# One row of statistics for the feed-forward: a product of ones with 256 columns, and a power on GpSimd over the row

## The chip, the cores and the metric

The kernel runs on one core of a Trainium2 chip. The metric is the device time of one execution in microseconds, the median of several. The engines are TensorE (PE in the rows, PEld for its weight loads), VectorE (DVE), ScalarE (ACT), GpSimd (POOL) and SyncE (SP), which issues transfers here.

## The reference

Two models run one after the other on 256 tokens of width 1024. The first has two layers, each with a feed-forward, a mixer of three branches and a second feed-forward; the second model has two layers of another mixer. The change touches the four feed-forwards:

```python
def rms_norm(x, g):
    y = xf * lax.rsqrt(jnp.mean(xf * xf, axis=-1, keepdims=True) + EPS)
    return (y * g.astype(jnp.float32)).astype(x.dtype)

def swiglu(h, w1, w3, w2):
    return (jax.nn.silu(h @ w1) * (h @ w3)) @ w2

for l in range(DEPTH):
    x = x + 0.5 * swiglu(rms_norm(x, ffn1_norm[l]), ffn1_w1[l], ffn1_w3[l], ffn1_w2[l])
    ...
    x = x + 0.5 * swiglu(rms_norm(x, ffn2_norm[l]), ffn2_w1[l], ffn2_w3[l], ffn2_w2[l])
```

Everything is float32.

## The kernel before

The activations lie transposed: `xT` has 128 channels on the partitions, in 8 chunks, and the 256 tokens as columns. A product in near float32 is made of three matmuls: `xh`, `xl` are the high part and the remainder of the activations, `H`, `L` those of the weights.

Weights arrive as slabs of 128x1024 in five buffers `raw`, issued by SyncE. For each slab ScalarE makes `H` (L329) and VectorE makes `L = raw - H` (L333), with three buffers each, about two slabs ahead of TensorE. One slab gives 24 matmuls of 256 columns (L429 to L431: `H` with `xh`, `H` with `xl`, `L` with `xh`).

The feed-forward (`ffn`) has 22 blocks `f`. Each takes two slabs, one for the columns of `w1` and one for those of `w3`, into one PSUM tile (`col2`); a task `gated` then makes `t = p * rb` on VectorE (L589), `u = silu(t)` on ScalarE (L591), `w = p * u` on VectorE (L594), and the high part and remainder `gh`, `gl` of it. So the factor 1/rms of each token, `rb`, is multiplied in only after the product, and TensorE can start before it is known. The first three or four blocks use PSUM tiles of the pool `pa`, so that several can wait for `rb`; the others use `pd`.

`rb` is a 128x256 tile, the same row of 256 factors on all partitions. `stats` makes it from `ss`, the sums of squares per partition and token: a product with one column of ones for each half of the tokens (L477), the mean and epsilon on VectorE (L480, `ms`), a power of -0.5 on GpSimd for 128x2 numbers (L481, `m`), two diagonal matrices `dg` on VectorE (L486), their products with a matrix of ones (L490), and a copy to SBUF on ScalarE (L492, `rb`). The mixers use `m` too; the feed-forward uses `rb` alone.

The order on each engine is the order in which the Python code issues instructions; nothing reorders it. Tasks are generators: `spawn` puts one in a list with a delay, `tick` (called after every four chunks of a product) runs the tasks that are due, and `yield n` puts a task off by n ticks. `gated` waits in this list, and not on an engine, until the task of the statistics has ended; from then on it issues at most one block every two ticks.

Of the kernel before, what the change touches and what calls it, by code (L numbers as in the profile page):

```python
# [14 lines left out]
OP = mybir.AluOpType  # L15
AX = mybir.AxisListType

P = 128
T = 256
D = 1024  # L20
# [4 lines left out]
EPS = 1e-6  # L25
# [235 lines left out]
class Kernel:  # L261
# [208 lines left out]
    def stats(s, delay=4):  # L470
# [23 lines left out]
        s.stat = s.spawn(run(), delay)  # L494
        return s.stat


    def group(s, cols, per, evac):

        ps = [s.D(), s.D()]  # L500
        for k0 in range(0, KD, per):
            H, L = s.take()
            for tb in range(2):
                o, t = ps[tb][:, :cols], tok(tb)
                for kk in range(per):
                    k, c = k0 + kk, slice(kk * cols, (kk + 1) * cols)
                    s.T.matmul(o, s.xh[:, k, t], H[:, c], start=(k == 0), stop=False)  # L507
                    s.T.matmul(o, s.xh[:, k, t], L[:, c], start=False, stop=False)  # L508
                    s.T.matmul(o, s.xl[:, k, t], H[:, c], start=False, stop=(k == KD - 1))  # L509
                if cols > 300 or tb:  # L510
                    s.tick()
                if k == KD - 1 and not tb:
                    ev = s.begin(evac(ps))
        return ev
# [60 lines left out]


    def ffn(s, nextg, delay=5, late=True, early=4):
        s.stats(delay)
        gh = [s.B4("gh", [P, 4, T], F32R) for _ in range(6)]
        gl = [s.B4("gl", [P, 4, T], F32R) for _ in range(6)]  # L580

        s.gate = 0

        def gated(f, p):
            while s.busy([s.stat]) or s.now < s.gate:
                yield 1
            s.gate = s.now + 2
            t = s.K2("t256", [P, T])
            s.V.tensor_tensor(t, p[:, :T], s.rb, OP.mult)  # L589
            u = s.K2("u256", [P, T])  # L590
            s.A.activation(u, t, AF.Silu)  # L591
            yield 1
            w = s.K2("w256", [P, T])
            s.V.tensor_tensor(w, p[:, T:], u, OP.mult)  # L594
            yield from s.split_late(gh[f // 4][:, f % 4], gl[f // 4][:, f % 4], w)

        for f in range(NF):
            s.begin(gated(f, s.col2(late and f == 0, s.S() if f < early else None)))
        for m in range(KD):
            p = s.D()  # L600
            for k0, n in W2CUT:
                H, L = s.take()
                for kk in range(n):
                    k, a = k0 + kk, slice(kk * P, (kk + 1) * P)
                    s.mm3(p[:, :T], H[:, a], L[:, a], gh[k // 4][:, k % 4], gl[k // 4][:, k % 4], k == 0, k == NF - 1)
                    if kk in (3, n - 1):
                        s.tick()
            t = s.K2("t256", [P, T])
            s.V.tensor_tensor(t, p[:, :T], s.rb, OP.mult)
            s.V.scalar_tensor_tensor(s.xT[:, m], t, 0.5, s.xT[:, m], OP.mult, OP.add)  # L610
            nextg(m)
# [1208 lines left out]
```

## Time and profile before

| | |
|---|---|
| median of 3 runs | 1560.76 us (1560.53 to 1562.33) |
| the profiled execution | 1562.33 us, span 1560.6 us |
| TensorE busy | 1542.4 us, 99% of the span |
| VectorE busy | 1097.4 us, 70% |
| ScalarE busy | 876.0 us, 56% |
| GpSimd busy | 202.6 us, 13% |

The span goes from the first to the last instruction. Busy time is the time in which an engine has an instruction running; matmuls overlap, so their durations add up to more than the time that they take.

### The profile page before, as it was taken

To read this page: it belongs to the slowest core of one execution; us is meant where nothing else is said; L and a number is where in the kernel's file an instruction comes from. 1 tells how busy PE (TensorE), PEld (TensorE's weight loads), DVE (VectorE), ACT (ScalarE), POOL (GpSimd) and SP (SyncE) were. 2 spreads that over 40 slices of the span, in tenths; PEclk is the share of its full clock that TensorE was granted. 3 is DMA by queue.
4 is the path that set the end of the run, shared out by engine and by line. 5 is a ranking of instruction groups with operands and counts; after the bars stand their busy time and mean duration, and the time that the engine had idled before them with its cause. 6 is when DMAs were issued, how large, how long until landed. Compare 5 with 4: busy or idle time off the path is not lost.

```text
span 1560.6 us, 30856 instructions
## 1 busy us (share of the span) xinstructions
PE 1542.4 (99%) x12470; PEld 1452.7 (93%) x12470; DVE 1097.4 (70%) x1838; ACT 876.0 (56%) x1487; POOL 202.6 (13%) x248
## 2 busy tenths in 40 slices
PE   8999999999999999999999999999999999999998
PEld 8999987889999999999998888999999988888887
DVE  5766667667776666666667766777666689868985
ACT  5554466654564554554446765455544446864685
POOL 2000042311020000000013241102000022112200
PEclk9999999999999999999999999999999999999999
DMA  7555653533555556555665453455556573347331
GB/s 262 188 195 184 204 192 141 184 114 137 193 197 191 194 178 198 202 190 191 185 203 185 148 178 123 146 190 191 190 195 192 195 292 118 116 152 266 113 102 55
DMA packets 78128, 275.93 MB, mean 177 GB/s; under 512 B 8769, under 2 KB 8913, under 8 KB 77985
## 3 DMA queue, kind: packets, MB, share of 16 engines
q1 hardware_dynamic: 75744, 266.60, 49.8%
q0 software_dynamic: 1520, 6.22, 1.2%
q8 instruction: 98, 1.61, 0.4%
q10 hardware_dynamic: 720, 1.13, 0.2%
q14 instruction: 46, 0.37, 0.1%
HBM read 272.87 MB, written 1.05 MB: 176 GB/s over the span
## 4 chain that ended last, share of the span: by engine, by line
PE 88%; DVE 7%; ACT 2%; issue 1%; DMA 0%; ACTq 0%; POOL 0%; POOLq 0%
PE pd L429 21%; PE pd L430 20%; PE pd L431 20%; PE pd L507 4%; PE pd L508 4%; PE pd L509 4%; DVE L L333 2%; PE pa L431 2%; PE pa L430 2%; PE pa L429 2%; DVE nab L1235 2%; PE pa L446 1%; PE pa L700 1%; PE pa L679 1%; DVE xl L453 1%
## 5 line engine op out<-in xcount | busy, mean ns | idle before, releaser
L333 DVE TENSOR_TENSOR L<-raw,H 128x1024 fp32r<-128x1024 f32 (+2 forms) x490 | 595.1, 1221 | 215.4 <-ACT H L329 213.8
L329 ACT ACTIVATE H<-raw 128x1024 fp32r<-128x1024 f32 (+2 forms) x490 | 501.4, 1031 | 279.5 <-PE pd L430 95.5
L429 PE MATMUL pd<-xh,H 128*128 128x256 f32 x1856 | 519.8, 280 | 0.0
L431 PE MATMUL pd<-xh,L 128*128 128x256 f32 x1856 | 513.1, 276 | 0.3 <-DVE L L333 0.3
L430 PE MATMUL pd<-xl,H 128*128 128x256 f32 x1856 | 512.9, 276 | 0.0
L429 PEld LDWEIGHTS pd<-xh,H 128*128 128x128 f32 x1856 | 348.4, 188 | 8.1 <-issue 5.3
L431 PEld LDWEIGHTS pd<-xh,L 128*128 128x128 f32 x1856 | 348.5, 188 | 0.5 <-DVE L L333 0.5
L430 PEld LDWEIGHTS pd<-xl,H 128*128 128x128 f32 x1856 | 348.6, 188 | 0.3
L431 PE MATMUL pd<-gh,L 128*128 128x256 f32 x704 | 194.3, 276 | 0.0
L429 PE MATMUL pd<-gh,H 128*128 128x256 f32 x704 | 194.3, 276 | 0.0
L430 PE MATMUL pd<-gl,H 128*128 128x256 f32 x704 | 194.3, 276 | 0.0
L466 POOL TENSOR_TENSOR ss<-ss,sq 128x512 f32<-128x512 f32 x22 | 34.0, 1544 | 853.8 <-issue 566.0
L429 PEld LDWEIGHTS pd<-gh,H 128*128 128x128 f32 x704 | 132.2, 188 | 0.0
L430 PEld LDWEIGHTS pd<-gl,H 128*128 128x128 f32 x704 | 132.2, 188 | 0.0
L431 PEld LDWEIGHTS pd<-gh,L 128*128 128x128 f32 x704 | 132.2, 188 | 0.0
L591 ACT ACTIVATE u<-t 128x256 f32<-128x256 f32 x88 | 36.7, 417 | 165.1 <-DVE t L589 165.1
L507 PE MATMUL pd<-H,xh 128*128 128x512 f32 (+1 forms) x320 | 127.8, 399 | 0.0
L508 PE MATMUL pd<-L,xh 128*128 128x512 f32 (+1 forms) x320 | 122.2, 382 | 1.4 <-DVE L L333 1.4
L509 PE MATMUL pd<-H,xl 128*128 128x512 f32 (+1 forms) x320 | 122.0, 381 | 0.0
L452 ACT ACTIVATE xh<-xT,prm 128x256 fp32r<-128x256 f32 x64 | 30.6, 504 | 96.1 <-DVE xT L610 87.2
L507 PEld LDWEIGHTS pd<-H,xh 128*128 128x128 f32 x320 | 60.1, 188 | 14.5 <-issue 3.4
L508 PEld LDWEIGHTS pd<-L,xh 128*128 128x128 f32 x320 | 60.3, 188 | 12.4 <-DVE L L333 2.3
(419 smaller groups left out, 2615.3 us busy)
## 6 DMA issues: line engine op xcount, KB each, us to landing
raw<-in_f SPq DMA_DIRECT2D x206, 512.0 KB, 3.9
raw<-in_f SPq DMA_DIRECT2D x64, 448.0 KB, 3.6
raw<-in_mA SPq DMA_DIRECT2D x56, 512.0 KB, 3.2
raw<-in_mG SPq DMA_DIRECT2D x48, 512.0 KB, 3.2
raw<-in_hB SPq DMA_DIRECT2D x36, 512.0 KB, 3.3
raw<-in_mB SPq DMA_DIRECT2D x24, 512.0 KB, 3.2
raw<-in_mO SPq DMA_DIRECT2D x16, 512.0 KB, 3.3
cwt<-in_cw SPq DMA_DIRECT2D x16, 512.0 KB, 6.4
```

What stands on the lines that cost most here:

```text
L329: s.A.activation(H[:, a], raw[:, a], AF.Copy, **({} if g is None else {"scale": g}))
L333: s.V.tensor_tensor(L[:, a], raw[:, a], H[:, a].bitcast(F32), OP.subtract)
L429: s.T.matmul(out, lh, rh, start=start, stop=False)
L430: s.T.matmul(out, lh, rl, start=False, stop=False)
L431: s.T.matmul(out, ll, rh, start=False, stop=stop)
L452: s.A.activation(s.xh[:, k], s.xT[:, k], AF.Copy, scale=g[:, k:k + 1])
L466: s.G.tensor_tensor(s.ss, s.ss, q, OP.add)
L507: s.T.matmul(o, s.xh[:, k, t], H[:, c], start=(k == 0), stop=False)
L508: s.T.matmul(o, s.xh[:, k, t], L[:, c], start=False, stop=False)
L509: s.T.matmul(o, s.xl[:, k, t], H[:, c], start=False, stop=(k == KD - 1))
L591: s.A.activation(u, t, AF.Silu)
L1235: s.V.scalar_tensor_tensor(acc[:, c], y, w, acc[:, c], OP.mult, OP.add)
```

## The change

`ffn` calls `stats_row` in the place of `stats`. It makes the sums on all partitions at once, by one product of the matrix of ones with the 256 columns of `ss`, then the mean and epsilon for 128x256 numbers on VectorE, and the power for 128x256 numbers on GpSimd, in place, with the exponent broadcast. There is no `m`, no diagonal matrix, no second product and no copy on ScalarE. The task ends one tick earlier than before. The mixers keep `stats`.

```diff
+    def stats_row(s, delay):
+
+        rb = s.rb = s.W("rb", [P, T])
+
+        def run():
+            p = s.S()
+            s.T.matmul(p[:, :T], s.ones, s.ss[:, :T], start=True, stop=True)
+            yield 1
+            s.V.tensor_scalar(rb, p[:, :T], 1.0 / D, EPS, OP.mult, OP.add)
+            s.G.tensor_tensor(rb, rb, s.mhalf[:, :1].broadcast_to([P, T]), OP.pow)
+            yield 2
+        s.stat = s.spawn(run(), delay)
+        return s.stat
 
     def ffn(s, nextg, delay=5, late=True, early=4):
-        s.stats(delay)
+        s.stats_row(delay)
```

The new lines shift the later ones by 14: `t` is L603 in the changed kernel, `u` L605, `w` L608, `gl` L1155.

VectorE at the start of the first feed-forward, before (each name carries a running number):

```order
L333 TENSOR_TENSOR L_334<-raw_300,H_333 128x1024
L480 TENSOR_SCALAR ms_383<-pa_362 128x2
L333 TENSOR_TENSOR L_369<-raw_331,H_368 128x1024
L486 TENSOR_SCALAR dg_399<-ident_76,m_149 128x128 x2
L333 TENSOR_TENSOR L_405<-raw_366,H_404 128x1024
L589 TENSOR_TENSOR t256_436<-pa_163,rb_150 128x256
L594 TENSOR_TENSOR w256_458<-pa_163,u256_438 128x256
```

and now:

```order
L333 TENSOR_TENSOR L_333<-raw_299,H_332 128x1024
L505 TENSOR_SCALAR rb_149<-pa_361 128x256
L333 TENSOR_TENSOR L_367<-raw_330,H_366 128x1024
L603 TENSOR_TENSOR t256_413<-pa_162,rb_149 128x256
L333 TENSOR_TENSOR L_399<-raw_364,H_398 128x1024
L608 TENSOR_TENSOR w256_430<-pa_162,u256_415 128x256
L603 TENSOR_TENSOR t256_451<-pa_231,rb_149 128x256
```

The first `t` stood behind two `L` after the statistics, and now stands behind one.

VectorE at the start of the second feed-forward (the third and the fourth read the same), before:

```order
L333 TENSOR_TENSOR L_5437<-raw_5427,H_5436 128x1024
L480 TENSOR_SCALAR ms_5467<-pa_5451 128x2
L486 TENSOR_SCALAR dg_5487<-ident_76,m_5358 128x128 x2
L333 TENSOR_TENSOR L_5473<-raw_5434,H_5472 128x1024
L589 TENSOR_TENSOR t256_5525<-pa_5372,rb_5359 128x256
L333 TENSOR_TENSOR L_5510<-raw_5470,H_5509 128x1024
L594 TENSOR_TENSOR w256_5542<-pa_5372,u256_5527 128x256
```

and now:

```order
L333 TENSOR_TENSOR L_5426<-raw_5416,H_5425 128x1024
L505 TENSOR_SCALAR rb_5348<-pa_5440 128x256
L333 TENSOR_TENSOR L_5460<-raw_5423,H_5459 128x1024
L603 TENSOR_TENSOR t256_5487<-pa_5361,rb_5348 128x256
L608 TENSOR_TENSOR w256_5509<-pa_5361,u256_5489 128x256
L333 TENSOR_TENSOR L_5495<-raw_5457,H_5494 128x1024
L603 TENSOR_TENSOR t256_5525<-pa_5420,rb_5348 128x256
```

One `L` stands between the statistics and `t` in both; the next `L` now has `w` ahead of it.

ScalarE at the same place, before:

```order
L329 ACTIVATE H_5472<-raw_5434 128x1024
L329 ACTIVATE H_5509<-raw_5470 128x1024
L492 ACTIVATE rb_5359<-pa_5503 128x256
L591 ACT_TABLE_LOAD
L591 ACTIVATE u256_5527<-t256_5525 128x256
L329 ACTIVATE H_5546<-raw_5507 128x1024
```

and now:

```order
L329 ACTIVATE H_5459<-raw_5423 128x1024
L605 ACT_TABLE_LOAD
L605 ACTIVATE u256_5489<-t256_5487 128x256
L329 ACTIVATE H_5494<-raw_5457 128x1024
L1153 ACTIVATE gh_5349<-w256_5509 128x256
L605 ACTIVATE u256_5527<-t256_5525 128x256
```

Two `H` stood ahead of the first `u`; one of them, the `H` of the slab after next, has moved behind it.

## Rows read from the trace of the kernel before

**Rows 1.** The page: busy time of the engines, and TensorE's granted clock by slices.

```profile
PE 1542.4 (99%) x12470; PEld 1452.7 (93%) x12470; DVE 1097.4 (70%) x1838; ACT 876.0 (56%) x1487; POOL 202.6 (13%) x248
...
PEclk9999999999999999999999999999999999999999
```

**Rows 2.** Waits of TensorE: total us, times, longest; the first of ten.

```profile
PE pa L1430 <- DVE kcz L1424: 3.3, 2, 1.7
```

**Rows 3.** GpSimd's groups by shape (count, busy us, mean ns), then its timeline.

```profile
L466 POOL TENSOR_TENSOR ss<-ss,sq 128x512 f32<-128x512 f32 x22 | 34.0, 1544 | 853.8 <-issue 566.0 <-ACT sq L464 287.8
...
L440 POOL TENSOR_TENSOR r<-r,mhalf 128x4 f32<-128x4 f32 x14 | 14.4, 1025 | 1.2
...
250.65 0.21 POOL L439 TENSOR_SCALAR r<-ss 128x16 f32<-128x16 f32 x1 [5.54 <-DVE ss L626]
250.94 3.94 POOL L440 TENSOR_TENSOR r<-r,mhalf 128x16 f32<-128x16 f32 x1
...
281.39 1.11 POOL L439 TENSOR_SCALAR r<-ss 128x16 f32<-128x16 f32 x1 [26.51 <-DVE ss L626]
282.59 2.90 POOL L440 TENSOR_TENSOR r<-r,mhalf 128x16 f32<-128x16 f32 x1
```

**Rows 4.** Timeline of the first feed-forward's start, engine by engine: start, duration in us.

```profile
28.28 0.36 PE L429 MATMUL pd<-xh,H 128*128 128x256 f32 x1
...
32.49 0.60 PE L490 MATMUL pa<-dg,ones 128*128 128x128 f32 x4
32.85 0.36 PE L429 MATMUL pd<-xh,H 128*128 128x256 f32 x1
...
36.02 0.28 PE L429 MATMUL pd<-xh,H 128*128 128x256 f32 x1
...
37.04 0.28 PE L429 MATMUL pd<-xh,H 128*128 128x256 f32 x1
...
28.45 0.16 DVE L480 TENSOR_SCALAR ms<-pa 128x2 f32<-128x2 f32 x1 [0.85 <-PE pa L477]
...
33.55 0.42 DVE L589 TENSOR_TENSOR t<-pa,rb 128x256 f32<-128x256 f32 x1
...
35.55 1.23 DVE L333 TENSOR_TENSOR L<-raw,H 128x1024 fp32r<-128x1024 f32 x1 [0.66 <-ACT H L329]
...
28.70 0.72 POOL L481 TENSOR_TENSOR m<-ms,mhalf 128x2 f32<-128x2 f32 x1 [3.38 <-DVE ms L480]
...
34.01 0.42 ACT L591 ACTIVATE u<-t 128x256 f32<-128x256 f32 x1 [0.49 <-DVE t L589]
34.45 1.07 ACT L329 ACTIVATE H<-raw 128x1024 fp32r<-128x1024 f32 x1
```

**Rows 5.** Timeline of the second feed-forward's start: TensorE, then VectorE.

```profile
458.25 0.50 PE L477 MATMUL pa<-ones,ss 128*128 128x1 f32 x4
458.61 0.36 PE L429 MATMUL pa<-xh,H 128*128 128x256 f32 x1
...
459.65 0.15 DVE L480 TENSOR_SCALAR ms<-pa 128x2 f32<-128x2 f32 x1
...
464.27 0.42 DVE L589 TENSOR_TENSOR t<-pa,rb 128x256 f32<-128x256 f32 x1 [1.76 <-ACT rb L492]
464.61 1.22 DVE L333 TENSOR_TENSOR L<-raw,H 128x1024 fp32r<-128x1024 f32 x1
```

**Rows 6.** Instructions of one line, L1474: ns min/median/max of a record.

```profile
L1474 PE MATMUL pa<-big,lb x16: 377/379/403, 1305.8 to 1461.2; 128*128 128x256 f32 x16
```

**Rows 7.** TensorE's timeline early in the run; then windows, the granted clock third from last.

```profile
10.52 0.38 PE L429 MATMUL pa<-xh,H 128*128 128x256 f32 x1 [1.40 <-ACT xh L452]
...
12.00:13.00 1.00, 1.00 (x7) 1.00 (x7) 1.00 (x3) 1.00 (x3) 0.00 (x0) 0.50 1.05 418
...
11.00:16.00 5.00, 4.75 (x26) 4.75 (x27) 4.71 (x9) 5.00 (x9) 0.26 (x1) 0.66 1.02 404
```

## The prediction

> **What bounds the kernel now.** I read the page first. TensorE is busy 99% of the span, and its granted clock reads 9 tenths or more in each of the forty slices [rows 1]. The list of waits, taken for TensorE alone, confirms that nothing else sets the time: its longest entry is 3.3 us in total [rows 2]. So the span is TensorE's work, and the other engines matter only where they are late for it. Two consequences follow. Something that takes work off VectorE, ScalarE or GpSimd gains nothing. And a time in which TensorE stands still is not given back later, because there is no other idle time that it could be moved into. What has to be found is therefore the deadline by which each result of the changed code is wanted, and who stands in the queue behind the instruction that wants it.
>
> **What the change removes and adds.** It acts four times, at the start of each of the four feed-forward stages.
>
> TensorE loses two products of one column and two of 128 columns. Each pair costs 0.36 us of its stream (32.49 to 32.85 for the second pair; the first shows the same between 458.25 and 458.61) [rows 4, 5]. It gains one fp32 product of 256 columns. Such a product takes two records of about 0.38 us [rows 6], so between 0.36 us (the price of the two 128-column ones) and 0.76 us. The balance per stage is between 0.36 us saved and 0.04 us lost: at most 1.4 us over all four.
>
> VectorE loses 0.16 us for `ms` and the two `dg` products, and gets one 128x256 operation that reads PSUM; the nearest row is the 128x256 product `t` at 0.42 us [rows 4]. ScalarE loses one copy. Both engines have idle time there, so I count these at nothing beyond the 0.42 us in the chain.
>
> GpSimd's power goes from 2 columns to 256. The trace has powers of three widths: 2 columns 0.72 us, 4 columns 1.025 us, 16 columns 2.90 or 3.94 us [rows 3, 4]. Other GpSimd work is far cheaper per column: the 512-column sum takes 1.54 us, 3.0 ns a column [rows 3]. From 2 to 4 columns the power costs 0.155 us a column, and from 4 to the shorter 16 it costs (2.90 - 1.025) / 12 = 0.156. Three widths lie on one line. The longer time of 16 columns follows a scale-and-shift of 0.21 us, the shorter one a scale-and-shift of 1.11 us; the two pairs last about the same (4.2 and 4.1 us) [rows 3], so the extra microsecond seems not to be the power's own. I take 2.90 + 240 x 0.157 = 40.6 us for 256 columns. The upper bound goes through 3.94: (3.94 - 1.025) / 12 = 0.243 a column, 3.94 + 240 x 0.243 = 62 us. The lower bound is the price of the ordinary sum, 256 x 3.0 ns = 0.8 us. These ends are far apart; I take the line, because it is drawn through the same operation at three widths.
>
> The Trainium skill, GPSIMD Engine Reference, section "Elementwise — side-by-side cycle accounting", gives about 2.6 cycles per element for a tensor-tensor operation, measured with additions (4497 ns for 2048 columns). By that page the row of 256 would be an estimated 0.6 us. The additions of this trace agree with the page (3.0 ns a column for 512); its powers do not, at some 156 ns a column, and for a power the rows decide.
>
> **Where the stall goes.** The order of the instructions shows it. In the first stage VectorE's `t` now stands before the second weight remainder `L` that follows the statistics, and waits for GpSimd. TensorE can work through the slab whose `L` stands ahead of `t`, and then two matmuls (they need only `H`) of the next. VectorE and ScalarE take their instructions in the written order, so no later `L` can be made while `t` waits.
>
> Stage 1: the statistics reach VectorE at 28.45 [rows 4]. Add 0.42 for the operation and 0.09 to GpSimd's start (the step from 28.45 + 0.16 to 28.70): the power starts at 28.96 and ends at 69.6. `t` starts then, `L` 0.34 us after it (464.27 to 464.61 shows this step), and lasts 1.23: TensorE can go on at 71.2. In the run of before it came to that matmul 74 matmuls after 28.28. Nine of them take 1.02 us (36.02 to 37.04) [rows 4, 5], which makes 0.1135 each and 8.4 us; with 0.36 for the `dg` product and 0.1 for the start that is 37.1. **Delay 34.1 us.**
>
> Stage 2: here not only `L` but also `H` of the next slab stands behind `t`: ScalarE has `u` ahead of that `H`, VectorE has `w` ahead of that `L`. The statistics reach VectorE at 459.65 [rows 5]; power from 460.16 to 500.8; `u` starts 0.46 after `t` (33.55 to 34.01), `H` 0.44 after `u` (34.01 to 34.45), `L` 1.10 after `H` (34.45 to 35.55) and lasts 1.23 [rows 4]: TensorE goes on at 504.0. Before, it came there 86 matmuls after 458.61, with 0.36 for `dg`: 468.7. **Delay 35.3 us.** Stages 3 and 4 have the same order on all engines; I take 35.3 for each.
>
> Sum of the four: 34.1 + 3 x 35.3 = 140.0 us.
>
> The clock comes on top. Early in the run TensorE waits, 1.40 us at the longest, and the granted clock then falls to 0.50, the lower level of 1.2 GHz; over 11 to 16 us it averages 0.66 with the engine busy 4.75 of these 5 us [rows 7]. That is 0.34 x 5 = 1.7 us of work lost before it is back. An idle time of 35 us should cost that each time: 4 x 1.7 = 6.8. A second price may follow the stall: VectorE and ScalarE come out of it with no lead. One slab costs TensorE 24 x 0.1135 = 2.7 us, and the chain `t`, `u`, `H`, `L` about 3.2 us for the first few; but the half clock slows TensorE in just these slabs, so I count nothing, and up to 5 us a stage in the range.
>
> 140.0 + 6.8 = 147 us. The profiled execution took 1562.33 us around its span of 1560.6; the median of the three is 1560.76. From the median: **1708 us**, 9.4% longer.
>
> **The rivals.**
> *The power is hidden* (the other side). If GpSimd took the long row at the price of its sums, `rb` would be ready before anyone wants it. The deadline decides: in stage 1 the power must end by 35.1 (6.1 us long), in stages 2 to 4 by 500.8 less 35.3 and the 0.36 of `dg`, that is 465.1 (4.9 us long). Below 4.9 us, 20 ns a column, nothing waits and only TensorE's balance is left: 1559.4 to 1561, no change that can be told. For it speaks only that the widths seen are all small; against it, that the price per column does not fall from 2 to 16. The page named above is the rule by which it would come out so; by the powers of this trace it does not hold.
> *The long row is cheaper per column, but not cheap*: 10 to 34 us. Then each stage loses the power's length less 5 or 6 us, plus the clock: 20 us would give 1708 - 4 x 20.6 = 1626.
> *The 3.94 us are the true price*: 62 us, 21.7 more in each stage, 1708 + 87 = 1795.
> *The recovery is slow*: the power is as forecast, but TensorE waits for some slabs after each stall. Up to 5 us a stage, 1728.
>
> **How the numbers follow.** The forecast with its slow recovery gets 0.72, and its own range is 1690 to 1735. The longer power 0.11, the middling one 0.08, the hidden one 0.09. Inside the hidden case a gain of over 0.2% (3.1 us, about what can be told from no change here) needs more than TensorE's 1.4 us; I leave 0.01 for it. So faster 0.01, same 0.08, slower 0.91. The range is 1640 to 1800: it takes in the upper bound of the power and the upper part of the middling case, and leaves out the hidden one.
>
> **What would show it.** The profile of the changed kernel should have four GpSimd powers of about 40 us, and TensorE idle for about 34 us in each of four places, released by `L` in the first and by `H` and then `L` in the others; VectorE waiting for GpSimd at `t`; a granted clock at half for a few microseconds after each; and everything between the stages as before. The prediction is wrong if those powers last under 5 us, or if they are long and TensorE is still not idle, which would mean that I misread which `L` is the last ahead of `t`.

## The result, and the profile after

The changed kernel takes 1728.59 us (median of 4 runs, 1728.25 to 1729.61), the kernel before 1560.76: a ratio of 1.1064, 95% interval 1.105 to 1.1077. The forecast was 1708 us in a range of 1640 to 1800, slower with a chance of 0.91. The profiled execution has a span of 1726.5 us, 165.9 more than the 1560.6 of before.

The page of the changed kernel, the lines that answer to [rows 1]:

```profile
PE 1569.6 (91%) x12446; PEld 1478.2 (86%) x12446; DVE 1095.3 (63%) x1830; ACT 875.1 (51%) x1483; POOL 367.6 (21%) x248
...
PEclk9699999999996999959999999999599999999999
```

TensorE is busy 91% of the span, and its granted clock is low in four slices. GpSimd has 165 us more work. TensorE's waits (total us, times, longest) and the power's own row (ns min/median/max) say where it went:

```profile
PE pa L429 <- ACT H L329: 104.9, 4, 34.9
PE pd L431 <- DVE L L333: 34.9, 1, 34.9
PE pa L1444 <- DVE kcz L1438: 3.3, 2, 1.7
PE pa L431 <- DVE L L333: 1.6, 4, 0.5
```

```profile
L506 POOL TENSOR_TENSOR rb<-rb,mhalf x4: 41127/41154/41158, 27.6 to 1203.7; 128x256 f32<-128x256 f32 x4
```

Four powers of 41.15 us, and four times in which TensorE stands still for 34.8 to 34.95 us: three released by `H` from ScalarE, one by `L` from VectorE. Nothing else that TensorE waits for has grown much since [rows 2]. The timeline of the first two places, engine by engine (start, duration in us, in brackets the idle time before and what ended it), shows the queue:

```profile
27.10 0.42 DVE L505 TENSOR_SCALAR rb<-pa 128x256 f32<-128x256 f32 x1 [0.94 <-PE pa L503]
27.64 1.66 DVE L333 TENSOR_TENSOR L<-raw,H 128x1024 fp32r<-128x1024 f32 x1
...
27.61 41.16 POOL L506 TENSOR_TENSOR rb<-rb,mhalf 128x256 f32<-128x256 f32 x1 [1.79 <-DVE rb L505]
...
68.80 0.42 DVE L603 TENSOR_TENSOR t<-pa,rb 128x256 f32<-128x256 f32 x1 [39.50 <-POOL rb L506]
69.14 1.22 DVE L333 TENSOR_TENSOR L<-raw,H 128x1024 fp32r<-128x1024 f32 x1
...
70.41 0.58 PE L431 MATMUL pd<-xh,L 128*128 128x256 f32 x1 [34.95 <-DVE L L333]
...
541.19 0.43 DVE L603 TENSOR_TENSOR t<-pa,rb 128x256 f32<-128x256 f32 x1 [38.87 <-POOL rb L506]
542.10 0.42 DVE L608 TENSOR_TENSOR w<-pa,u 128x256 f32<-128x256 f32 x1 [0.48 <-ACT u L605]
543.04 1.23 DVE L333 TENSOR_TENSOR L<-raw,H 128x1024 fp32r<-128x1024 f32 x1 [0.52 <-ACT H L329]
...
541.65 0.42 ACT L605 ACTIVATE u<-t 128x256 f32<-128x256 f32 x1 [39.29 <-DVE t L603]
541.97 1.04 ACT L329 ACTIVATE H<-raw 128x1024 fp32r<-128x1024 f32 x1
...
543.06 0.58 PE L429 MATMUL pa<-xh,H 128*128 128x256 f32 x1 [34.83 <-ACT H L329]
544.32 0.58 PE L431 MATMUL pa<-xh,L 128*128 128x256 f32 x1 [0.46 <-DVE L L333]
```

In the first stage one `L` gets through beside the power, then VectorE sits 39.5 us at `t`, and the next `L` and TensorE follow `t` at once. In the second the chain is `t`, `u`, `H`, and TensorE starts with `H`, to wait another 0.46 us for `L`.

That makes 34.95 + 34.83 + 34.87 + 34.84 = 139.5 us of the 165.9, and 1.4 us in the three short waits behind `H`. Part of the rest is the clock. Windows of 10 us from the end of each idle time (busy time of the engines, granted clock third from last):

```profile
70.41:80.41 10.00, 10.00 (x71) 10.00 (x72) 8.60 (x17) 6.01 (x12) 0.00 (x0) 0.80 0.64 209
543.06:553.06 10.00, 9.54 (x60) 9.24 (x61) 7.89 (x13) 5.15 (x10) 0.00 (x0) 0.71 0.46 159
764.00:774.00 10.00, 9.53 (x56) 9.24 (x57) 7.74 (x12) 4.78 (x9) 0.00 (x0) 0.66 0.48 159
1246.75:1256.75 10.00, 9.54 (x61) 9.24 (x62) 8.09 (x13) 5.35 (x10) 0.00 (x0) 0.74 0.46 159
```

The clock's shortfall is 2.0, 2.9, 3.4 and 2.6 us; half of the idle time inside each window (0.46 us in the last three) comes off, which leaves some 10.2 us of work lost to the lower level of 1.2 GHz. 139.5 + 1.4 + 10.2 = 151.1. Some 15 us of the 165.9 are still missing.

The short falls of the clock away from the stalls do not explain them. The early one of [rows 7] is not in this trace, though TensorE waits at the same place, and one of the same size (0.28 x 6 = 1.7 us) stands late in the run instead, behind a wait of 1.66 us; the two cancel.

```profile
10.44 0.39 PE L429 MATMUL pa<-xh,H 128*128 128x256 f32 x1 [1.57 <-ACT xh L452]
...
10.00:20.00 10.00, 9.23 (x75) 8.97 (x76) 7.98 (x12) 8.73 (x14) 3.66 (x2) 1.00 0.98 378
1483.00:1489.00 6.00, 5.86 (x32) 5.58 (x32) 4.84 (x17) 3.97 (x13) 0.00 (x0) 0.72 0.25 91
```

The missing 15 us lie far from the stalls. In the second half of each feed-forward, the down projection, one block of 66 matmuls (one pass of its loop) ends with `xl` of its channels on VectorE. Two of these in a row, of the changed kernel and then of the kernel before:

```profile
904.01 0.48 DVE L453 SCALAR_TENSOR_TENSOR xl<-xT,prm,xh 128x256 fp32r<-128x256 f32 x1 [0.58 <-ACT xh L452]
911.83 0.48 DVE L453 SCALAR_TENSOR_TENSOR xl<-xT,prm,xh 128x256 fp32r<-128x256 f32 x1 [0.58 <-ACT xh L452]
```

```profile
784.15 0.48 DVE L453 SCALAR_TENSOR_TENSOR xl<-xT,prm,xh 128x256 fp32r<-128x256 f32 x1 [0.58 <-ACT xh L452]
791.63 0.48 DVE L453 SCALAR_TENSOR_TENSOR xl<-xT,prm,xh 128x256 fp32r<-128x256 f32 x1 [0.58 <-ACT xh L452]
```

A block takes 7.82 us where it took 7.48: 0.34 / 66 = 5 ns more for each matmul, with no wait between them. The records of these matmuls say the same (ns min/median/max), changed and before:

```profile
L429 PE MATMUL pd<-gh,H x704: 278/281/288, 167.4 to 1415.3; 128*128 128x256 f32 x176
```

```profile
L429 PE MATMUL pd<-gh,H x704: 276/276/276, 132.2 to 1251.9; 128*128 128x256 f32 x176
```

Four stages of eight blocks make 32 x 0.34 = 10.9 us; the matmuls of the mixers that read `yh` and `mh` are longer in the same way (medians of 282 ns where they were 276). The program offers a difference: `m` and `dg` are now first allocated in a mixer, behind `gh`, `gl` and `rb`. In the built program `gh` therefore begins at byte 111168 of a partition in the place of 111232, and with it `rb`, all tiles that share the buffers of `gh` (`gl`, `mh`, `ml`, `yh`, `yl`) and the small work tiles lie 64 bytes lower, while `xh`, `xl`, `H` and `L` stay where they were.

### The profile page after: what moved, and what is told of

The parts are those of the page before. It is cut to its first block, busy times and chain, and to the rows that moved or that the text cites. A ratio compares the mean times of both kernels' runs of the same rounds, so it can differ in the third digit from the quotient of the medians.

```text
span 1726.5 us, 30792 instructions
## 1 busy us (share of the span) xinstructions
PE 1569.6 (91%) x12446; PEld 1478.2 (86%) x12446; DVE 1095.3 (63%) x1830; ACT 875.1 (51%) x1483; POOL 367.6 (21%) x248
## 4 chain that ended last, share of the span: by engine, by line
PE 82%; POOL 10%; DVE 4%; ACT 1%; issue 1%; DMA 1%; POOLq 0%; ACTq 0%; SPq 0%
PE pd L429 19%; PE pd L431 19%; PE pd L430 19%; POOL rb L506 10%; PE pd L521 4%; PE pd L522 4%; PE pd L523 4%; PE pa L431 1%; DVE L L333 1%; PE pa L714 1%; PE pa L429 1%; DVE nab L1249 1%; PE pa L430 1%; PE pa L446 1%; PE pa L693 1%
## 5 line engine op out<-in xcount | busy, mean ns | idle before, releaser
L431 PE MATMUL pd<-xh,L 128*128 128x256 f32 x1856 | 515.5, 278 | 34.9 <-DVE L L333 34.9
L431 PEld LDWEIGHTS pd<-xh,L 128*128 128x128 f32 x1856 | 350.1, 189 | 35.3 <-DVE L L333 35.1
L605 ACT ACTIVATE u<-t 128x256 f32<-128x256 f32 x88 | 36.7, 417 | 324.7 <-DVE t L603 324.7
L429 PE MATMUL pd<-gh,H 128*128 128x256 f32 x704 | 198.7, 282 | 0.0
L431 PE MATMUL pd<-gh,L 128*128 128x256 f32 x704 | 198.5, 282 | 0.0
L429 PE MATMUL pa<-xh,H 128*128 128x256 f32 x240 | 71.1, 296 | 106.4 <-ACT H L329 104.9
L506 POOL TENSOR_TENSOR rb<-rb,mhalf 128x256 f32<-128x256 f32 x4 | 164.6, 41148 | 8.5 <-PE pa L431 3.6
L429 PEld LDWEIGHTS pa<-xh,H 128*128 128x128 f32 x240 | 48.5, 202 | 107.6 <-ACT H L329 105.7
```

The source lines that it names most:

```text
L429: s.T.matmul(out, lh, rh, start=start, stop=False)
L431: s.T.matmul(out, ll, rh, start=False, stop=stop)
L506: s.G.tensor_tensor(rb, rb, s.mhalf[:, :1].broadcast_to([P, T]), OP.pow)
```

## The experiments

The theory for the idle time is the forecast's: `t` waits for a power that costs some 0.16 us a column, and `L` and `H` stand behind it. For the rest, two theories: the places of the tiles in SBUF, or a slow recovery after each stall.

**The tiles back at their places.**

```diff
     def stats_row(s, delay):
+        s.W("m", [P, 2])
         rb = s.rb = s.W("rb", [P, T])
         def run():
             p = s.S()
+            s.W("dg", [P, 2, P], bufs=1)
```

> The changed kernel, with the tiles m and dg reserved (but not written) by the row version at the places in the allocation order that they had before, so that the tiles gh, gl, mh, ml, yh, yl and the small work tiles lie at the SBUF addresses of the kernel before; in the changed kernel they lie 64 bytes lower. Theory (placement): the matmuls of the down projection and of the mixers' projections that read these tiles run some 5 ns slower each because of the new addresses, about 15 us of the 168; they return to 276 ns and 7.48 us per block of the down projection, and the time is 1713 to 1715 us. Rival (slow recovery): what is left over beside the four idle times comes from VectorE and ScalarE running without a lead after each stall; then addresses change nothing and the time stays within 1727 to 1730 us.

Measured: 1714.03 us (1712.8 to 1715.21), ratio 1.0961 (1.0942 to 1.098) where the changed kernel has 1.1064. The span is 1713.1 us, 13.4 less. The idle times are as before (104.9 us in four waits for `H`, the one of stage 1 35.0 us), and the matmuls of the down projection are back:

```profile
L429 PE MATMUL pd<-gh,H x704: 275/276/277, 168.8 to 1403.2; 128*128 128x256 f32 x176
```

Two reservations that the row version neither writes nor reads take the loss away. The slow recovery falls: all stalls are still there, and the sum closes. Windows from the end of each idle time of this run:

```profile
71.83:81.83 10.00, 10.00 (x71) 10.00 (x72) 8.69 (x17) 6.00 (x12) 0.00 (x0) 0.80 0.69 202
539.84:549.84 10.00, 9.54 (x55) 9.24 (x55) 7.74 (x12) 4.64 (x9) 0.00 (x0) 0.65 0.48 158
758.72:768.72 10.00, 9.53 (x56) 9.24 (x57) 7.74 (x12) 4.86 (x9) 0.00 (x0) 0.67 0.47 158
1236.69:1246.69 10.00, 9.53 (x57) 9.24 (x58) 7.74 (x12) 4.91 (x9) 0.00 (x0) 0.68 0.45 158
```

By the same reckoning the clock takes 11.3 us here, and 139.5 + 1.4 + 11.3 = 152.2 of the 152.5 us that this span is above the 1560.6 of before.

**Half of the power.** 128 columns; the other 128 tokens get a factor of one.

```diff
-            s.V.tensor_scalar(rb, p[:, :T], 1.0 / D, EPS, OP.mult, OP.add)
-            s.G.tensor_tensor(rb, rb, s.mhalf[:, :1].broadcast_to([P, T]), OP.pow)
+            s.V.tensor_scalar(rb[:, :128], p[:, :128], 1.0 / D, EPS, OP.mult, OP.add)
+            s.G.tensor_tensor(rb[:, :128], rb[:, :128], s.mhalf[:, :1].broadcast_to([P, 128]), OP.pow)
+            s.V.tensor_scalar(rb[:, 128:], p[:, 128:T], 0.0, 1.0, OP.mult, OP.add)
```

> The changed kernel with the power over 128 of the 256 columns; the other 128 are filled with ones by VectorE, so half of the tokens are left without their factor. Theory (the queue waits for a power that costs 0.16 us a column): the power takes 20.5 to 21 us, TensorE's four idle times fall from 35 to about 14.7 us each, and the time is 1728.6 less 4 x 20.3, 1645 to 1650 us. Rival (the row has a fixed price, or the idle time is set by something else): less than half of that, above 1690 us.

Measured: 1647.23 us (1645.38 and 1649.09), ratio 1.0536 (1.051 to 1.0562). The power, and TensorE's two first waits:

```profile
L506 POOL TENSOR_TENSOR rb<-rb,mhalf x4: 20729/20753/20759, 30.7 to 1145.1; 128x128 f32<-128x128 f32 x4
```

```profile
PE pa L429 <- ACT H L329: 43.2, 4, 14.3
PE pd L431 <- DVE L L333: 14.4, 1, 14.4
```

The power is 20.4 us shorter and each idle time 20.5 us shorter: beyond its slack, every microsecond of the power is a microsecond of TensorE.

**`t` later in the queue.** The evacuation of stages 2 to 4 starts eight ticks later, so that four more `L` and `H` are ahead of `t`; the power is untouched.

```diff
-            yield 2
+            yield 10 if delay == 5 else 2
```

> The changed kernel with the evacuation held back by eight more ticks in the stages 2 to 4, so that four more weight remainders L and their H stand ahead of the first t on VectorE and ScalarE. The power is as long as before. Theory (the deadline is set by what stands behind t in the queues): TensorE can work through four more slabs of 2.72 us, the idle times of these three stages fall from 35 to 24 us, the time is 1728.6 less 32.6, 1693 to 1699 us; stage 1 stays at 35 us. Rival (TensorE waits for the factor itself or for the PSUM tiles): the idle times stay at 35 us and the time above 1724 us.

Measured: 1696.67 us (1696.41 and 1696.93), ratio 1.0852 (1.0829 to 1.0875).

```profile
PE pd L429 <- ACT H L329: 71.9, 3, 24.0
PE pd L431 <- DVE L L333: 36.3, 4, 34.9
```

Three idle times of 24.0 us, one still of 34.9 in stage 1: 10.9 us less for four slabs of 2.72 us. What stands behind `t` sets the idle time, and neither the factor itself nor the PSUM tiles.

**A power that is hidden.** As the half, with 16 columns; 240 tokens get a factor of one.

```diff
-            s.G.tensor_tensor(rb, rb, s.mhalf[:, :1].broadcast_to([P, T]), OP.pow)
+            s.G.tensor_tensor(rb[:, :16], rb[:, :16], s.mhalf[:, :1].broadcast_to([P, 16]), OP.pow)
+            s.V.tensor_scalar(rb[:, 16:], p[:, 16:T], 0.0, 1.0, OP.mult, OP.add)
```

> The changed kernel with the power over 16 of the 256 columns; the other 240 are filled with ones by VectorE, so these tokens are left without their factor. The power should take 2.9 us, less than the 4.9 us of slack, so nothing waits. Theory (placement): only the shifted addresses remain as a loss, 1573 to 1577 us against 1560.8. Rival (slow recovery): with no stall there is nothing to recover from, and the time is 1559 to 1562 us.

Measured: 1577.84 us (1575.47 to 1580.34), ratio 1.0092 (1.0073 to 1.0111); the kernel before took 1564.11 us on this chip.

```profile
L506 POOL TENSOR_TENSOR rb<-rb,mhalf x4: 2906/2922/2927, 30.6 to 1092.4; 128x16 f32<-128x16 f32 x4
```

A power of 2.92 us makes nobody wait, and 13.7 us are lost all the same, with no stall to recover from.

**The same at the old places.** The edit above together with the first one.

> As the 16-column power (240 tokens without their factor, power hidden), with m and dg reserved at their old places so that the tiles lie at the addresses of the kernel before. Theory (placement): the 15 us go away, 1559 to 1563 us, no difference from the kernel before. Rival (the loss of the 16-column run is something else in the row version, such as the fp32 product of 256 columns): the time stays at 1575 to 1580 us.

Measured: 1561.91 us (1560.24 to 1562.6) beside 1562.78, ratio 0.9993 (0.9983 to 1.0002). So the loss was the places, and the row's product on TensorE costs nothing that can be told.

**The kernel before, shifted.** An unused tile, nothing else:

```diff
         m, rb = s.m, s.rb = s.W("m", [P, 2]), s.W("rb", [P, T])
+        s.W("gap", [P, 56])
```

> The kernel before, with nothing changed but an unused pair of tiles of 56 floats reserved behind rb, which moves gh, gl, mh, ml, yh, yl and the small work tiles up by 448 bytes, that is to the same place modulo 512 bytes as in the changed kernel. Theory (what matters is where these tiles lie relative to each other and to H and L within 512 bytes): slower by some 15 us, 1573 to 1579 us, the down projection 5 ns a matmul slower. Rival (the absolute distance of 64 bytes, or something in the changed program): no difference, 1560 to 1563 us.

Measured: 1578.93 us (1576.79 to 1579.22) beside 1562.78, ratio 1.0101 (1.0084 to 1.0117).

```profile
L429 PE MATMUL pd<-gh,H x704: 279/281/287, 131.1 to 1265.2; 128*128 128x256 f32 x176
```

The kernel of before gets the same loss from 448 bytes upwards as the changed one from 64 downwards. The change's own instructions have no part in it, and neither has the place of `rb`, which did not move here.

**A row without the power.** A square root on ScalarE and a reciprocal on VectorE, at the old places; all of the computation is there.

```diff
-            s.G.tensor_tensor(rb, rb, s.mhalf[:, :1].broadcast_to([P, T]), OP.pow)
+            s.A.activation(rb, rb, AF.Sqrt)
+            s.V.reciprocal(rb, rb)
```

> The row version with a square root on ScalarE and a reciprocal on VectorE in the place of the power, at the old addresses; it computes all that the reference does. Theory: rb is ready about 3 us after the statistics, nothing waits, and TensorE saves 0 to 0.4 us a stage for its one product instead of four: 1559 to 1562 us, no change that can be told. Rival (two more function table loads of about 1.3 us each stand in ScalarE's queue ahead of H, so that TensorE waits): 1564 to 1572 us.

Measured: 1561.89 us (1560.11 to 1563.12, 11 runs) beside 1562.78 (20 runs), ratio 0.9994 (0.9985 to 1.0003). The second stage's start, VectorE and then ScalarE:

```profile
459.93 1.75 DVE L509 RECIPROCAL rb<-rb 128x256 f32<-128x256 f32 x1 [0.49 <-ACT rb L508]
461.60 1.16 DVE L333 TENSOR_TENSOR L<-raw,H 128x1024 fp32r<-128x1024 f32 x1
462.68 0.41 DVE L606 TENSOR_TENSOR t<-pa,rb 128x256 f32<-128x256 f32 x1
...
457.05 1.28 ACT L508 ACT_TABLE_LOAD   x1
459.48 0.42 ACT L508 ACTIVATE rb<-rb 128x256 f32<-128x256 f32 x1 [1.15 <-DVE rb L507]
```

`t` starts at 462.68, earlier than in [rows 5] (464.27), and nothing comes of it, since TensorE did not wait there. The two more table loads (1.28 us at 457.05) make TensorE wait for nothing either: its longest entry in the list of waits is again 3.3 us in total. This is the row idea with all of its computation at the time of the kernel before; it does not beat it.

## Why the prediction was right, and where it was short

*The power.* 40.6 us were forecast by the line through 2, 4 and 16 columns; 41.15 were measured, and the three widths of the row version, 2.92, 20.75 and 41.15 us, lie on one line of 0.159 us a column: (20.75 - 2.92) / 112 and (41.15 - 20.75) / 128. The price per column does not fall with length, and the 16 columns of the row version take 2.92 and not the 3.94 us of [rows 3]; what made those longer stays open. The rival of a hidden power fell with it. The figure that the Trainium skill's GPSIMD Engine Reference, section "Elementwise — side-by-side cycle accounting", gives for an addition (about 2.6 cycles an element) does not carry over to a power; the trace of before already said so. For additions the forecast said that this trace agrees with the Trainium skill's page. That holds for the size alone: by the 4497 ns for 2048 columns of the Trainium skill's page a column takes an estimated 2.2 ns, and in the 512 columns of this trace it took 3.0.

*The queue.* Forecast: delays of 34.1 and three times 35.3 us, 140.0 together. Measured: idle times of 139.5 and short waits of 1.4. The half power and the later `t` show both halves of the mechanism, the length of the power and the place of `t`.

*The clock.* 1.7 us a stage were forecast from the one fall early in the run; 2.0 to 3.2 were lost, 10.2 in all where 6.8 stood. The term was there and too small. It rested on a single short fall behind a wait of 1.40 us, and such a fall did not even come back at the same place: behind 1.57 us there the clock of the changed kernel reads 1.00.

*The recovery.* I had left up to 5 us a stage for VectorE and ScalarE running without a lead. The waits of TensorE after the first `L` show none of it, and the run with the tiles at their places, which keeps all four stalls, leaves 0.3 us for it. This rival's 1728 is the measured time to within a microsecond, by a different cause.

*What was missing* is the step "What the change removes and adds": I costed instructions and left out that a tile allocated later moves the tiles behind it. So one of the forecast's signs did not come: between the stages not everything was as before. The move costs 13.4 us between the spans with and without it (1726.5 and 1713.1; the run without it lost 1.1 us more to the clock), 13.7 at a hidden power, 16 in the kernel before. Against the run with the tiles at their places the forecast is 6 us low, against the changed kernel 21 us.

## What to carry to other kernels

Price an operation by the rows of that operation: a GpSimd power cost over 50 times as much per column as a GpSimd sum in the same trace, and two or three widths were enough to draw the line. Then find what is queued behind the first instruction that reads its result, since with in-order engines the whole excess over that slack lands on the engine that sets the time. And when a change drops or moves an allocation, compare the addresses of the tiles: here 64 bytes in SBUF were worth 1% of the run.

## What the runs showed of the hardware

Matmuls of 256 columns that read `gh`, `gl`, `mh` or `yh` as the moving operand went from a record of 276 ns to about 281, and from 7.48 to 7.82 us a block, when these tiles moved by 64 bytes down or 448 up, which is the same place modulo 512 bytes. Why is open. The runs tell that the place decides. In the built programs `gh`, `xh`, `xl`, `H` and `L` all begin 128 bytes past a multiple of 512 where these matmuls take 276 ns, and `gh` begins 64 bytes past one in both slower places; whether it is the distance to the other tiles or the place by itself that counts, and whether modulo 512 or only modulo 128, the runs do not separate. Which of the moved tiles matter, and with which other access they meet (the weights `H` and `L`, the writes of VectorE and ScalarE, the transfers), was not tried.

After an idle time of 35 us the granted clock took unequal times to come back: from the end of the idle time the four windows read 0.80, 0.71, 0.66 and 0.74, that is 4.0, 5.8, 6.8 and 5.2 us at half.

One `L` that ran beside the beginning of the power took 1.66 us instead of 1.22 (27.64 above). It is a single row, of no consequence here: in the second stage the `L` beside the power took 1.23 (at 501.09).
